# Each weight slab's hi and lo tiles at other places within 256 bytes, low activation parts moved by 64 or 128 bytes

## The chip, the cores and the metric

One NeuronCore of one Trainium2 chip runs the kernel. The metric is device time in microseconds, the median over runs. Engines: PE (TensorE, with PEld for its weight loads), DVE (VectorE), ACT (ScalarE), POOL (GpSimd), SP (SyncE, which issues most DMAs).

## What is computed

One decoder layer for 256 tokens of width 2048, everything in float32:

```
hn = rmsnorm(x)
p  = hn @ w_in + b_in                      # 2048 x 6152
u  = silu(group_norm(causal_dwconv(p[ca] * sigmoid(p[cg]))))
q, k = silu(causal_dwconv(p[q, k])); v, o = p[v], sigmoid(p[o])
hm = group_norm(mlstm(q, k, v, gates)) * o
x  = x + concat(u, hm) @ w_out             # 2048 x 2048
up = rmsnorm(x) @ w_up                     # 2048 x 11264
x  = x + (silu(causal_dwconv(up[gate])) * up[rest]) @ w_down   # 5632 x 2048
out = rmsnorm(x)
```

## The kernel before, in words

Weights stream through SBUF in 400 slabs of 256 rows (two blocks of 128, the index k) by up to 512 columns. SP loads a slab into a tile raw (`load`, L185 on). A float32 slab is then split into two float32r tiles: ACT casts it to hi (L219), and DVE, or POOL for some slabs of the input projection, subtracts to make lo = raw - hi (L224). hi and lo have four buffers each, made in `split_tiles` (L201 on), and are made three slabs ahead of their use. The activations are split in the same way: xp (input projection) and x1p (gate and up) hold high and low parts in one tile, mixh and mixl (output projection) and ah and al (down projection) are two tiles each. A product is then hi x high + hi x low + lo x high, each a float32r matmul with its own weight load on PE.

Which operand streams and which is loaded as weights differs by stage:

- conv gate (slabs 0 to 31) and q and k (56 to 87), `ws_group`, L254: hi or lo is loaded as weights (128 columns), 256 columns of xp stream. 24 matmuls per slab.
- o projection (slabs 32 to 55) and v projection (88 to 103), `xs_group`, L298 to L300: 128 columns of xp are loaded, hi or lo streams, 344 columns for o and 512 for v. 12 matmuls per slab.
- output projection (104 to 135), the same lines: mixh or mixl is loaded, 512 columns of hi or lo stream. 12 per slab.
- gate and up (136 to 311), `wp_group`: hi is loaded and 512 columns of x1p (high and low parts together) stream (L279), then lo is loaded and 256 columns stream (L280). 16 per slab.
- down projection (312 to 399), L298 to L300, and for the last block of columns `down_last` (L850 to L852): ah or al is loaded, 512 columns of hi or lo stream (256 at the very end). 12 per slab.

The order of all instructions is written by hand: a loop over the slabs issues one slab's load, a later slab's split, this slab's matmuls, and the small tasks due at this slab (`after`, `tasks`). The program as built gives each tile a fixed address within a partition. Modulo 256 bytes, all hi and lo tiles start at 160, xp and x1p at 192, mixh, mixl, ah and al at 160. The steps between the column blocks of hi and lo and between the blocks of activations are multiples of 512 bytes, except in the o projection, where the second block of a slab starts 1376 bytes after the first. Parameters come in seven transposed row tiles (`load_rows`, L111 on) with a tag of their own.

Of the kernel before, what the change touches and what calls it, by code (L numbers as in the profile page):

```python
# [9 lines left out]
F32 = mybir.dt.float32  # L10
F32R = mybir.dt.float32r
# [4 lines left out]
P = 128  # L16
# [15 lines left out]
W = 512  # L32

RAW_BUFS = 5
SPLIT_BUFS = 4
AHEAD = 3
SIG = 4
WARM = (6, 5)
BY_K = 3


@with_exitstack
def hybrid_layer_kernel(
# [6 lines left out]
    nc = tc.nc  # L50
    act, dve, pool, pe = nc.scalar, nc.vector, nc.gpsimd, nc.tensor
# [28 lines left out]


    mixh = mid.tile([P, NK, T], F32R, tag="mixh", name="mixh")
    mixl = mid.tile([P, NK, T], F32R, tag="mixl", name="mixl")


# [21 lines left out]
    warm = cst.tile([P, 1], F32, tag="warm", name="warm")  # L107
    act.copy(warm, ones[:, 0:1])

    def load_rows(parts, name):  # L110
        n = sum(p[1] for p in parts)  # L111
        r = mid.tile([P, P], F32, tag="rows", name="rows_" + name, bufs=7)
        o = 0
        for ap, k in parts:
            nc.sync.dma_start(r[o:o + k, :], ap)
            o += k
        return r, n
# [4 lines left out]
    rows = {}  # L122
# [51 lines left out]

    raw_t, hi_t, lo_t = {}, {}, {}
    mid_hook = []

    def load(i):
        if i >= len(slabs):
# [20 lines left out]
    def split_tiles(i):  # L200
        s = slabs[i]  # L201
        n = s["nk"] * s["w"]
        raw = raw_t.pop(i)
        hi = slab.tile([P, 2 * W], F32R, tag="hi", name=f"hi{i}", bufs=SPLIT_BUFS)
        lo = slab.tile([P, 2 * W], F32R, tag="lo", name=f"lo{i}", bufs=SPLIT_BUFS)
        s["eng"] = pool if s["pool"] and i >= 8 and i % 2 else dve
        hi_t[i] = hi[:, :n].rearrange("p (k c) -> p k c", k=s["nk"])
        lo_t[i] = lo[:, :n].rearrange("p (k c) -> p k c", k=s["nk"])
        s["lo"] = 0.0 if s["eng"] is pool else 1.1 * n + 30
        return raw, hi, lo  # L210
# [15 lines left out]
    def w_slab(wap, kt, nk, col, w, fn, on_pool):  # L226
        if col is None:
            src = wap(kt)
        else:
            src = wap[kt * P:(kt + nk) * P, col:col + w].rearrange("(k p) c -> p k c", p=P)  # L230
        slabs.append(dict(src=src, w=w, nk=nk, mm=fn, pool=on_pool))


    def ws_group(wap, col, mov, nk, done, on_pool):
        st = {}

        def mk(kt):
            def fn(hi, lo):
                if kt == 0:
                    st["b"] = [mm_bank("ws0"), mm_bank("ws1")]  # L240
                mh, ml = mov()
                for k in range(2):
                    if mid_hook and mid_hook[0][0] == k:
                        mid_hook.pop(0)[1]()
                    hh, hl, lh = (hi, mh), (hi, ml), (lo, mh)
                    i = cur[0]
                    if i >= NK // 2:
                        steps = [(ct, a) for ct in range(4) for a in (hh, hl, lh)]
                    else:
                        steps = [(ct, a) for a in ((hh, lh, hl) if i + k == 0 else (hh, hl, lh)) for ct in range(4)]  # L250
                    for ct, (w, m) in steps:
                        o = v2(st["b"][ct // 2])[:, ct % 2, :]
                        first = kt + k == 0 and ct % 2 == 0 and w is hi and m is mh
                        pe.matmul(o, w[:, k, ct * P:(ct + 1) * P], m[:, kt + k, :], start=first,  # L254
                                  stop=kt + k == nk - 1 and w is lo, skip_group_check=True)
                if kt + 2 == nk:
                    done(st["b"])
            return fn

        for kt in range(0, nk, 2):  # L260
            w_slab(wap, kt, 2, col, W, mk(kt), on_pool)
# [43 lines left out]
    def xs_group(wap, col, w, stat, nk, done, on_pool):  # L305
        st = {}
        for kt in range(0, nk, 2):
            xs_slab(wap, col, w, stat, kt, kt == 0, kt + 2 == nk, st, done, on_pool)
# [39 lines left out]
    def done_ag(p):  # L348
        def fn(banks):
            sg = []  # L350

            def ev():
                for k in range(2):
                    c = 2 * p + k
                    act.activation(up[c][:, upos:], v2(banks[0])[:, k, :], AF.Identity, bias=bi[:, c:c + 1])
                sg.append(t2k("sg"))
                for k in range(2):
                    c = 2 * p + k
                    act.activation(v2(sg[0])[:, k, :], v2(banks[1])[:, k, :], AF.Sigmoid, bias=bi[:, 8 + c:9 + c])

            def mul():
                for k in range(2):
                    c = 2 * p + k
                    dve.tensor_mul(up[c][:, upos:], up[c][:, upos:], v2(sg[0])[:, k, :])
                conv_pair(p)
            d0 = 5 if p == 0 else 1
            after(d0, lambda: scale_banks(banks), 1300)
            after(d0 + 1, ev)
            after(d0 + 2, mul, 700)
        return fn  # L370
# [312 lines left out]
    def open_ffn():  # L683
        if "ah" in ffn:
            return
        inner.close()
        fp = ctx.enter_context(tc.tile_pool(name="ffn", bufs=1))
        ffn["pool"] = fp
        ffn["ah"] = fp.tile([P, NF, T], F32R, tag="ah", name="ah")
        ffn["al"] = fp.tile([P, NF, T], F32R, tag="al", name="al")  # L690
        ffn["gp"] = [fp.tile([P, 2, FK - 1 + T], F32, tag=f"gp{i}", name=f"gp{i}") for i in range(2)]
        for g in ffn["gp"]:
            pool.memset(g[:, :, 0:FK - 1], 0.0)
# [194 lines left out]


    ag = w_in[:, 0:2 * DC].rearrange("(k p) (s c) -> p k s c", p=P, s=2)  # L890
    for j in range(4):
        ws_group(lambda kt, j=j: ag[:, kt:kt + 2, :, T * j:T * (j + 1)], None, get_xT, NK, done_ag(j), True)
    for b in range(3):
        xs_group(w_in, OFF_O + OW * b, OW, get_xT, NK, done_o(b), True)
    for half in range(2):
        ws_group(w_in, OFF_Q + 512 * half, get_xT, NK, done_qk(0, half), True)
        ws_group(w_in, OFF_K + 512 * half, get_xT, NK, done_qk(1, half), True)

    at = defaultdict(list)
    v_start = len(slabs)  # L900
    for hp in range(2):
        xs_group(w_in, OFF_V + 512 * hp, W, get_xT, NK, done_v(hp), True)
    at[v_start - 2] += [(0, 0), (1, 1)]
# [3 lines left out]
        return mixh, mixl  # L907

    p3_start = len(slabs)
    sts = [{}, {}, {}, {"cv": True}]  # L910
    for n0 in (0, 2):
        for half in range(2):
            for n in (n0, n0 + 1):
                for kt in range(8 * half, 8 * half + 8, 2):
                    xs_slab(w_out, 512 * n, W, get_mix, kt, kt == 0, kt == 14, sts[n], done_out(n), False)

    for j in range(NF // 4):
        wp_group(w_up, 512 * j, done_gate(j), gate_banks)
        wp_group(w_up, DFF + 512 * j, done_up(j), up_banks)
    for n in range(3):  # L920
        xs_group(w_down, 512 * n, W, lambda: (ffn["ah"], ffn["al"]), NF, done_down(n, 512 * n, W), False)
    down_last(3, 1536, W, SPLIT_BUFS)
# [189 lines left out]
```

## Time and profile before

| | us |
|---|---|
| median of 2 runs | 1130.84 (1130.81 to 1130.87) |
| the profiled execution | 1131.08 |
| its span, first to last instruction | 1129.3 |
| PE busy, mean granted clock | 1118.7, 0.998 |
| DVE, ACT, POOL busy | 746.0, 578.9, 131.6 |

The profile is of one execution. Busy time on PE is no measure of its rate, since matmuls are pipelined; the distance between the starts of matmuls is.

### The profile page before, as it was taken

Reading aid. Unit: us, or ns where it says so; the run is one execution under the profiler, and the core shown is the slowest. Engines: PE = TensorE matmul, PEld = TensorE weight load, DVE = VectorE, ACT = ScalarE, POOL = GpSimd, SP = SyncE. Lnnn points to the kernel's source line nnn. Section 1 sums busy time; section 2 is a strip of 40 time slices with the busy share of each in tenths; the row PEclk is TensorE's granted clock in tenths of the full one; section 3 lists DMA queues with packets and bytes.
Section 4 is the critical chain, followed back from the end, with each engine's and each line's share of the span. In section 5 each row is a group of like instructions: output and inputs, shape, how many; then the busy total and the mean of one; then the engine's idle time right before and its main releaser. Section 6 shows DMA issues by size and latency. Waiting matters only on the chain.

```text
span 1129.3 us, 16955 instructions
## 1 busy us (share of the span) xinstructions
PE 1118.7 (99%) x6506; PEld 994.4 (88%) x6506; DVE 746.0 (66%) x1139; ACT 578.9 (51%) x823; POOL 131.6 (12%) x100
## 2 busy tenths in 40 slices
PE   9999999999999999999999999999999999999997
PEld 9999999998888888888888888888888888888886
DVE  5498999986765557657666666676576645454543
ACT  5745476754545455555545555455555444343433
POOL 0443554534200000000000000000000000000000
PEclk9999999999999999999999999999999999999999
DMA  8864665565655666666666666666666666666662
GB/s 262 272 190 125 193 205 186 175 183 166 218 192 184 173 195 190 192 188 185 188 199 191 184 191 189 194 188 192 188 186 188 197 193 230 197 188 196 191 195 89
DMA packets 122681, 215.40 MB, mean 191 GB/s; under 512 B 7440, under 2 KB 33256, under 8 KB 122088
## 3 DMA queue, kind: packets, MB, share of 16 engines
q1 hardware_dynamic: 121048, 209.92, 61.8%
q10 hardware_dynamic: 1552, 4.39, 1.0%
q8 instruction: 51, 0.84, 0.3%
q14 instruction: 30, 0.25, 0.1%
HBM read 212.19 MB, written 2.10 MB: 190 GB/s over the span
## 4 chain that ended last, share of the span: by engine, by line
PE 95%; DVE 3%; ACT 1%; issue 1%; DMA 0%; ACTq 0%; POOLq 0%; POOL 0%
PE ws L254 16%; PE gate L279 14%; PE up L279 14%; PE xs L298 9%; PE xs L299 9%; PE xs L300 9%; PE up L280 8%; PE gate L280 8%; PE xs L852 2%; PE xs L850 2%; PE xs L851 2%; DVE conv L386 2%; DVE lo L224 1%; DMA xs<-in_x_dram 0%; PE xT L940 0%
## 5 line engine op out<-in xcount | busy, mean ns | idle before, releaser
L224 DVE TENSOR_TENSOR lo<-raw,hi 128x1024 fp32r<-128x1024 f32 (+2 forms) x355 | 434.6, 1225 | 326.6 <-ACT hi L219 325.5
L219 ACT CAST hi<-raw 128x1024 fp32r<-128x1024 f32 (+2 forms) x401 | 411.5, 1030 | 452.4 <-PE xs L300 152.5
L279 PE MATMUL gate<-x1p,hi 128*128 128x512 f32 x704 | 245.0, 390 | 0.0
L279 PE MATMUL up<-x1p,hi 128*128 128x512 f32 x704 | 244.5, 390 | 0.0
L280 PE MATMUL up<-x1p,lo 128*128 128x256 f32 x704 | 198.5, 282 | 0.0
L280 PE MATMUL gate<-x1p,lo 128*128 128x256 f32 x704 | 198.5, 282 | 0.0
L254 PE MATMUL ws<-xp,hi 128*128 128x256 f32 x1024 | 178.5, 282 | 0.0
L279 PEld LDWEIGHTS up<-x1p,hi 128*128 128x128 f32 x704 | 132.2, 188 | 27.7
L279 PEld LDWEIGHTS gate<-x1p,hi 128*128 128x128 f32 x704 | 132.2, 188 | 27.6
L254 PEld LDWEIGHTS ws<-xp,hi 128*128 128x128 f32 x1024 | 153.4, 189 | 0.8 <-issue 0.3
L254 PE MATMUL ws<-xp,lo 128*128 128x256 f32 x512 | 135.5, 280 | 0.5 <-DVE lo L224 0.5
L280 PEld LDWEIGHTS gate<-x1p,lo 128*128 128x128 f32 x704 | 133.1, 189 | 0.0
L280 PEld LDWEIGHTS up<-x1p,lo 128*128 128x128 f32 x704 | 133.1, 189 | 0.0
L224 POOL TENSOR_TENSOR lo<-raw,hi 128x1024 fp32r<-128x1024 f32 (+1 forms) x48 | 111.1, 2317 | 148.2 <-ACT hi L219 142.2
L299 PE MATMUL xs<-lo,ah 128*128 128x512 f32 x264 | 102.7, 389 | 0.0
L300 PE MATMUL xs<-hi,al 128*128 128x512 f32 x264 | 102.7, 389 | 0.0
L298 PE MATMUL xs<-hi,ah 128*128 128x512 f32 x264 | 102.7, 389 | 0.0
L386 DVE SCALAR_TENSOR_TENSOR conv<-up,cB,conv 128x256 f32<-128x256 f32 x240 | 97.6, 478 | 0.0
L254 PEld LDWEIGHTS ws<-xp,lo 128*128 128x128 f32 x512 | 93.2, 189 | 0.9 <-DVE lo L224 0.7
L827 POOL TENSOR_TENSOR rf<-ms,halves 128x1 f32<-128x1 f32 x2 | 1.1, 550 | 711.7 <-DVE ms L821 711.7
L300 PEld LDWEIGHTS xs<-hi,al 128*128 128x128 f32 x264 | 49.6, 188 | 10.4
L298 PEld LDWEIGHTS xs<-hi,ah 128*128 128x128 f32 x264 | 49.6, 188 | 10.4
(186 smaller groups left out, 1204.5 us busy)
## 6 DMA issues: line engine op xcount, KB each, us to landing
raw<-in_w_up_dram SPq DMA_DIRECT2D x176, 512.0 KB, 3.9
raw<-in_w_down_dram SPq DMA_DIRECT2D x88, 512.0 KB, 4.7
raw<-in_w_in_dram SPq DMA_DIRECT2D x48, 512.0 KB, 4.4
raw<-in_w_in_dram SPq DMA_DIRECT2D x64, 256.0 KB, 4.6
raw<-in_w_out_dram SPq DMA_DIRECT2D x32, 512.0 KB, 4.6
raw<-in_w_in_dram SPq DMA_DIRECT2D x24, 344.0 KB, 3.4
x<-in_x_dram ACTq DMA_DIRECT2D x2, 1024.0 KB, 7.7
xs<-in_x_dram SPq DMA_DIRECT2D x7, 256.0 KB, 5.6
```

Of the source, the lines that this page charges most:

```text
L219: copy(hi[:, c], raw[:, c])
L224: slabs[i]["eng"].tensor_sub(lo[:, c], raw[:, c], hi[:, c].bitcast(F32))
L254: pe.matmul(o, w[:, k, ct * P:(ct + 1) * P], m[:, kt + k, :], start=first, stop=kt + k == nk - 1 and w is lo, skip_group_check=True)
L279: pe.matmul(o, hi[:, k, cs], m2, start=first, stop=last, skip_group_check=True)
L280: pe.matmul(o[:, 0:T], lo[:, k, cs], mp[:, kt + k, 0, :], start=False, stop=last, skip_group_check=True)
L298: pe.matmul(o, sh[:, kt + k, ts_], hi[:, k, :w], start=first and k == 0, stop=False)
L299: pe.matmul(o, sh[:, kt + k, ts_], lo[:, k, :w], start=False, stop=False)
L300: pe.matmul(o, sl[:, kt + k, ts_], hi[:, k, :w], start=False, stop=last and k == 1)
L386: dve.scalar_tensor_tensor(a, up[c][:, t:t + T], cB[:, 8 * t + c:8 * t + c + 1], a, op0=ALU.mult, op1=ALU.add)
L850: pe.matmul(o, sh[:, kt, ts_], hi[:, k, c:c + cw], start=kt == first, stop=False, skip_group_check=True)
L851: pe.matmul(o, sh[:, kt, ts_], lo[:, k, c:c + cw], start=False, stop=False, skip_group_check=True)
L852: pe.matmul(o, sl[:, kt, ts_], hi[:, k, c:c + cw], start=False, stop=kt == NF - 1, skip_group_check=True)
```

## The change

The tiles hi and lo get 64 spare elements (256 bytes), and each slab uses its hi and lo from an offset of its own within them. `place(base, *pairs)` sets for the slabs that follow a list of pairs (bytes for hi, bytes for lo) through which they go in turn; the base is 32 where the partner is xp or x1p and 0 where it is mixh or ah, so that a pair tells how many bytes, modulo 256, hi and lo lie behind that partner. Before, the pair is (224, 224) for stages with xp or x1p, and (0, 0) for the two others.

- conv gate, q and k: (192, 64) in every slab; o projection: (64, 64); v projection: (0, 0)
- output projection: the 32 pairs of MID, one per slab
- gate and up: the last 176 of the 192 pairs of ALL, one per slab: all multiples of 16 of which at least one is no multiple of 32
- down projection: the 88 pairs of MORE, one per slab

A tile gap of 16 elements stands between mixh and mixl, and one of 32 between ah and al, each with a memset on POOL: mixl now starts at 224 and al at 32, modulo 256. To make room, the row tiles of the parameters take thirds of the tiles pw, which the mLSTM scores use later.

```
     mixh = mid.tile([P, NK, T], F32R, tag="mixh", name="mixh")
+    gap = mid.tile([P, 16], F32, tag="gap", name="gap")
+    nc.gpsimd.memset(gap, 0.0)
     mixl = mid.tile([P, NK, T], F32R, tag="mixl", name="mixl")

+    row_tiles = []
     def load_rows(parts, name):
-        r = mid.tile([P, P], F32, tag="rows", name="rows_" + name, bufs=7)
+        if not row_tiles:
+            t = mid.tile([P, 384], F32, tag="pw", name="rows_" + name, bufs=4)
+            row_tiles.extend(t[:, c * P:(c + 1) * P] for c in (2, 1, 0))
+        r = row_tiles.pop()

+    def place(base, *pairs):
+        stage["base"], stage["from"], stage["pairs"] = base, len(slabs), pairs
+
+    def places():
+        h, l = stage["pairs"][(len(slabs) - stage["from"]) % len(stage["pairs"])]
+        return (stage["base"] + h) % 256 // 4, (stage["base"] + l) % 256 // 4
+
+    G16 = [16 * a for a in range(16)]
+    ALL = [(h, l) for h in G16 for l in G16 if h % 32 or l % 32]
+    MID = [(h, l) for h in (0, 64, 128, 192) for l in (0, 32, 64, 96, 128, 160, 192, 224)]
+    MORE = [(h, l) for h in (0, 16, 32, 64, 128, 144, 160, 192) for l in (0, 16, 32, 64, 80, 128, 144, 160, 192, 208, 240)]

-        hi = slab.tile([P, 2 * W], F32R, tag="hi", name=f"hi{i}", bufs=SPLIT_BUFS)
-        lo = slab.tile([P, 2 * W], F32R, tag="lo", name=f"lo{i}", bufs=SPLIT_BUFS)
+        hi = slab.tile([P, 2 * W + ROOM], F32R, tag="hi", name=f"hi{i}", bufs=SPLIT_BUFS)
+        lo = slab.tile([P, 2 * W + ROOM], F32R, tag="lo", name=f"lo{i}", bufs=SPLIT_BUFS)
+        hi, lo = (t[:, o:o + 2 * W] for t, o in zip((hi, lo), s["at"]))

-        slabs.append(dict(src=src, w=w, nk=nk, mm=fn, pool=on_pool))
+        slabs.append(dict(src=src, w=w, nk=nk, mm=fn, pool=on_pool, at=places()))

         ffn["ah"] = fp.tile([P, NF, T], F32R, tag="ah", name="ah")
+        gap = fp.tile([P, 32], F32, tag="gap", name="gap")
+        pool.memset(gap, 0.0)
         ffn["al"] = fp.tile([P, NF, T], F32R, tag="al", name="al")

+    place(FROM_X, (192, 64))        # conv gate
+    place(FROM_X, (64, 64))         # o
+    place(FROM_X, (192, 64))        # q, k
+    place(FROM_X, (0, 0))           # v
+    place(FROM_MIX, *MID)           # output
+    place(FROM_X, *ALL[16:])        # gate, up
+    place(FROM_MIX, *MORE)          # down
```

No instruction of PE, ACT, DVE or SP is added or moved; two of the four writes of pw on DVE now also name a DMA queue among their waits. On POOL the two memsets are added. The program before, POOL's first instructions of the kernel proper (ident is the identity for PE's transposes):

```order
L1107 UNCONDITIONAL_BRANCH
masks.py:197 MEMSET ident 128x128
masks.py:199 ISA
masks.py:199 AFFINE_SELECT ident<-ident 128x128
L322 MEMSET up_98 128x30
```

And the changed program at the same place:

```order
L1141 UNCONDITIONAL_BRANCH
L86 MEMSET gap 128x16
masks.py:197 MEMSET ident 128x128
masks.py:199 ISA
masks.py:199 AFFINE_SELECT ident<-ident 128x128
L347 MEMSET up_100 128x30
```

The memset of gap stands ahead of ident; the rest follows as before.

## Rows read from the trace of the kernel before

**Rows 1.** The page: span, busy time, granted clock in 40 slices (9: 90% or more).

```profile
span 1129.3 us, 16955 instructions
...
PE 1118.7 (99%) x6506; PEld 994.4 (88%) x6506; DVE 746.0 (66%) x1139; ACT 578.9 (51%) x823; POOL 131.6 (12%) x100
...
PEclk9999999999999999999999999999999999999999
```


**Rows 2.** Waits of PE: us in total, times, longest; first and last of four.

```profile
PE warm L968 <- POOL ident masks.py:199: 1.4, 1, 1.4
...
PE xs L299 <- DVE lo L224: 0.4, 1, 0.4
```


**Rows 3.** Stretches: us, busy (instructions) by engine, granted clock, DMA share, GB/s.

```profile
98.00:150.00 52.00, 51.09 (x339) 50.58 (x338) 46.80 (x109) 28.96 (x43) 24.32 (x16) 1.00 0.61 180
150.00:245.60 95.60, 95.60 (x801) 94.00 (x802) 89.92 (x185) 63.95 (x90) 47.80 (x28) 1.00 0.61 188
...
391.00:883.00 492.00, 492.00 (x2841) 436.11 (x2840) 329.44 (x444) 261.11 (x385) 1.93 (x4) 1.00 0.65 190
```


**Rows 4.** Timeline of PE, down projection: start, us, engine, line; 12 steps apart.

```profile
1081.68 0.39 PE L850 MATMUL xs<-hi,ah 128*128 128x512 f32 x1
...
1084.40 0.39 PE L850 MATMUL xs<-hi,ah 128*128 128x512 f32 x1
```


**Rows 5.** Timeline of PE, end of the down projection; 24 steps apart.

```profile
1115.68 0.28 PE L850 MATMUL xs<-hi,ah 128*128 128x256 f32 x1
...
1118.56 0.28 PE L850 MATMUL xs<-hi,ah 128*128 128x256 f32 x1
```


**Rows 6.** Timeline of PE, up projection; 16 steps apart.

```profile
469.91 0.39 PE L279 MATMUL up<-x1p,hi 128*128 128x512 f32 x1
...
472.68 0.39 PE L279 MATMUL up<-x1p,hi 128*128 128x512 f32 x1
```


**Rows 7.** Timeline of PE, q and k; 24 steps apart.

```profile
231.90 0.39 PE L254 MATMUL ws<-xp,hi 128*128 128x256 f32 x2
...
234.70 0.39 PE L254 MATMUL ws<-xp,hi 128*128 128x256 f32 x2
```


**Rows 8.** Timeline of PE, o projection; 24 steps apart.

```profile
120.87 0.32 PE L298 MATMUL xs<-hi,xp 128*128 128x344 f32 x1
...
124.62 0.32 PE L298 MATMUL xs<-hi,xp 128*128 128x344 f32 x1
```


**Rows 9.** Timeline of PE, v projection; 12 steps apart.

```profile
251.30 0.40 PE L298 MATMUL xs<-hi,xp 128*128 128x512 f32 x1
...
254.10 0.40 PE L298 MATMUL xs<-hi,xp 128*128 128x512 f32 x1
```


**Rows 10.** Timeline of PE, the scores, in plain float32.

```profile
241.69 1.02 PE L570 MATMUL S<-qkt 128*128 128x256 f32 x4
```


**Rows 11.** Groups by shape: line, tiles, count | busy us, mean ns | idle before.

```profile
L279 PE MATMUL gate<-x1p,hi 128*128 128x512 f32 x704 | 245.0, 390 | 0.0
...
L280 PE MATMUL gate<-x1p,lo 128*128 128x256 f32 x704 | 198.5, 282 | 0.0
L254 PE MATMUL ws<-xp,hi 128*128 128x256 f32 x1024 | 178.5, 282 | 0.0
...
L254 PE MATMUL ws<-xp,lo 128*128 128x256 f32 x512 | 135.5, 280 | 0.5 <-DVE lo L224 0.5
...
L570 PE MATMUL S<-qkt 128*128 128x256 f32 x16 | 4.1, 378 | 0.0
```


**Rows 12.** Groups from 391 to 883 us: the casts and the subtractions.

```profile
L224 DVE TENSOR_TENSOR lo<-raw,hi 128x1024 fp32r<-128x1024 f32 x178 | 217.6, 1223 | 159.6 <-ACT hi L219 159.5
...
L219 ACT CAST hi<-raw 128x1024 fp32r<-128x1024 f32 x178 | 186.8, 1051 | 214.6 <-PE gate L279 114.9 <-PE up L279 91.2 <-ACT s L741 6.9
```


**Rows 13.** Timeline of the start: POOL's memsets and the second transposes of x.

```profile
1.32 0.53 POOL L322 MEMSET up<- 128x30 f32 x8
...
5.46 0.66 PE L940 MATMUL xT<-ident,xs 128*128 128x128 f32 x2 [0.54 <-DMA xs<-in_x_dram]
```

More of the change, by code (lines that the diff above doesn't have):

```diff
@@ L39 @@
 BY_K = 3
+ROOM = 64
+FROM_X, FROM_MIX = 32, 0
 @with_exitstack
@@ L176, in hybrid_layer_kernel @@
     mid_hook = []
+    stage = {}
+    def place(base, *pairs):
[7 more added lines that the diff above has]
+    MORE = [(h, l) for h in (0, 16, 32, 64, 128, 144, 160, 192) for l in (0, 16, 32, 64, 80, 128, 144, 160, 192, 208, 240)]
     def load(i):
```

## The prediction

> **What bounds the kernel now.** I read the page first. TensorE (PE) is busy 99% of a span of 1129.3 us, its granted clock is full in all 40 slices, and no other engine passes 66% [rows 1]. The waits of PE come next: four rows, from 1.4 us at the start down to 0.4 us [rows 2]. Then the stretches [rows 3]: PE is busy nearly all of the time in each (51.09 of 52.00, 95.60 of 95.60, 492.00 of 492.00 us) at a granted clock of 1.00, the 2.4 GHz level; VectorE (DVE) is near full from 98 to 150 us (46.80 of 52.00) and from 150 to 245.6 us (89.92 of 95.60), and two thirds busy in gate and up. So the time is the sum of the matmuls' steps, and the question is how long a step is. A matmul's own duration (390 ns) says nothing, since matmuls are pipelined; the step from one start to the next does, so the timelines of PE are read last, first and last row of a run with the count between.
>
> Every float32r matmul loads new weights, so a step is the streamed columns plus something for that load. In the down projection twelve steps of 512 columns take 1084.40 - 1081.68 = 2.72 us, 226.7 ns each [rows 4]; at its end 24 steps of 256 columns take 2.88 us, 120.0 ns each [rows 5]. The difference, 106.7 ns for 256 columns, is one column per cycle at 2.4 GHz, and the remainder is 13.3 ns in both: I call it the gap. The gap by stage:
> - gate and up: 16 matmuls (eight of 512, eight of 256 columns) in 472.68 - 469.91 = 2.77 us, 173.3 ns each against 160.0 of columns: 13.3 ns [rows 6]
> - conv gate, q and k (L254): 24 of 256 columns in 234.70 - 231.90 = 2.80 us, 116.7 ns: 10.0 ns [rows 7]
> - o projection: 24 of 344 columns in 3.75 us, 156.2 ns against 143.3: 12.9 ns [rows 8]
> - v projection: 12 of 512 columns in 2.80 us, 233.3 ns: 20.0 ns [rows 9]
> - scores, in plain float32: four of 256 columns, start of the first to end of the last 1.02 us, one lasting 0.38: three steps in 0.64 us, some 214 ns; if two cycles go to a column (213.3 ns) the gap is some 1 ns [rows 10, 11].
>
> So the gap isn't one constant. The kernel as built puts hi and lo at byte 160 of 256, xp and x1p at 192, mixh, mixl, ah and al at 160. Projection v streams hi and lo past weights 32 bytes further on; the down projection does the same at distance 0 with the same shapes, and its gap is 6.7 ns smaller. This pair of rows is the one sign in the trace that places matter; that v runs beside the mLSTM is the other explanation. Gate (distance 224, gap 13.3) and L254 (distance 224, gap 10.0) show that the distance alone does not settle it.
>
> **The change part by part.** No instruction of PE, ACT or SP is added, removed or moved; only addresses are new. The steps that it touches: gate and up 4 x 704 = 2816 (L279 and L280, each for gate and for up; two of the four rows in [rows 11]), output 32 slabs x 12 = 384, down 1080 (three column blocks of 22 slabs x 12, the last block 288 with its halves), v 16 x 12 = 192, o 24 x 12 = 288, L254 1024 + 512 = 1536 [rows 11].
>
> 1. Gate and up. Each of the 176 slabs gets another pair out of (16, 128) to (240, 240), relative to x1p, at least one of the two off the multiples of 32. No row shows such a place. Bounds from the nearest rows: the gap of the scores, 1 ns, gives 2816 x -12.3 = -34.6 us; that of v, 20 ns, gives 2816 x 6.7 = +18.9 us. A mean over 176 pairs that run through the 256 bytes should lie where most rows lie, 10 to 13.3 ns; I take 13.3, the row of this very stage: 0.
> 2. Output and down. hi in four (output) or eight (down) places, lo in eight or eleven, and the low part of the activations 64 (mixl) or 128 (al) bytes behind. 1464 steps, now at 13.3 ns. Bounds as above: 1464 x -12.3 = -18.0 us and 1464 x 6.7 = +9.8 us. I take 13.3, since 36 of 88 pairs in down and all 32 in output stay on multiples of 32: 0.
> 3. Projection v. hi and lo go to the place of xp, distance 0, as in the down projection [rows 4]. 192 x (13.3 - 20.0) = -1.3 us. If the mLSTM beside it makes the gap, 0; if it falls to 1 ns, -3.6 us.
> 4. L254 (conv gate, q, k): hi 192 and lo 64 bytes behind xp in place of 224 both. No row shows these distances. Bounds: 1536 x -9 = -13.8 us and 1536 x 10 = +15.4 us. I take no change, 0. For q and k half of a gain would be lost: DVE is idle only 95.60 - 89.92 = 5.7 us there [rows 3] and makes most of the lo tiles.
> 5. o projection: hi and lo 64 bytes behind xp, 288 x (1 - 12.9) = -3.4 us to 288 x 7.1 = +2.0 us; DVE is idle 5.2 us of the 52.0 there [rows 3], and PE already waits for its lo once [rows 2], so a small gain can show as that wait. I take 0.
> 6. ACT and DVE write hi and lo at other places. In gate and up the cast takes 1051 ns and the subtraction 1223 ns per slab of 2.77 us [rows 12], off the path. The cover goes when DVE, busy 329.44 of 492.00 us [rows 3], gets 162.6 us more work over 178 slabs, 0.91 us each, so the subtraction would have to slow from 1.22 to 2.1 us. Cost 0.
> 7. Two memsets on POOL. The first stands ahead of ident, for which PE's warm-up waits; the eight memsets of 128x30 take 0.53 us, so one of 128x16 some 0.06 us. The first transposes go on to wait for x by DMA, 0.54 us at 5.46 us [rows 13], which hides it. The second, before gp's memsets in the first gate group, has no reader, and nothing stands behind it on POOL but gp's two and the last two rf. Cost 0.
> 8. The rows of parameters share the pw tiles; two of the scores' four writes also wait for a DMA of rows, which landed some 200 us before. Cost 0.
>
> Sum: -1.3 us on the profiled 1131.08 us (span 1129.3 and 1.8 around it) is 1129.8 us; against the median, 1130.84, it is 1129.5 us. That is the forecast: no change that counts. A measurement of this kernel can tell about 2%, 22.6 us, from no change; in gaps, 4280 steps of gate, up, output and down by 5.3 ns.
>
> [...]
>
> [...]
>
> **The rivals.**
> - A, slower: the places off the multiples of 32 meet the other stream more often. All gate and up steps and the 52 of 88 down slabs with such a place go to v's 20 ns: 2816 x 6.7 + 1080 x 52/88 x 6.7 = 18.9 + 4.3 = +23.2 us, 1154 us. It becomes slower by over 2% where these stages' mean gap passes 18.6 ns. For it: v's row shows that 20 ns occurs at a distance of only 32 [rows 9]. Against: in v every step has that one distance, and here each slab has another.
> - B, faster: the gap is a collision of weight load and stream which most places avoid, as the scores' 1 ns suggests [rows 10]. If half of the pairs avoid it: half of (34.6 + 18.0) = -26.3 us, with v's -1.3 us 1103 us. Against: the scores stream at half the rate, and no float32r row is under 10 ns.
> - C, the change does nothing: the gap is a fixed price of a float32r weight load, and v's is the mLSTM's doing. 1130.8 us. Against: the same shapes give 20.0 and 13.3 at a steady step in both.
>
> **How the numbers follow.** Forecast, places matter but average out: 0.58. C: 0.17. A: 0.12. B: 0.13. Forecast and C lie within 2%, 0.75; B is the chance of faster by over 2%, A of slower. Inside the forecast the mean gaps may lie 4 ns to either side: 4280 x 4 = 17 us, with L254's 5 us of gain or loss about 20 us. So the range is 1108 to 1150 us; it leaves out the far parts of A and B, some 0.18.
>
> **What would show it.** Right: gate slabs whose 16 steps differ from slab to slab, around 2.77 us in the mean; v at 2.72 us per slab; PE 99% busy and the four waits as before. Wrong: all gate slabs at 2.77 us still (C), a mean under 2.69 us (B) or over 2.86 us (A); or new waits of PE for lo, which would mean that ACT or DVE became slow at the new places. The prediction fails if the time is off by more than 20 us, or if v stays at 2.80 us, since then its one term that rests on a row is wrong.

## The result, and the profile after

The changed kernel takes 1139.45 us (two runs, 1138.45 to 1140.45) against 1130.84 before: 1.0079 times as long, 95% interval 1.0058 to 1.0099. That is 8.6 us more: less than the 2% that count as a change, but well outside the scatter. The forecast of "no change" missed a small, real loss.

The page of the changed kernel: span, busy time, granted clock in 40 slices.

```profile
span 1138.7 us, 16959 instructions
...
PE 1127.8 (99%) x6506; PEld 991.4 (87%) x6506; DVE 741.8 (65%) x1139; ACT 578.4 (51%) x823; POOL 133.4 (12%) x102
...
PEclk9999999999999999999999999999999999999999
```

Against [rows 1] the span is 9.4 us longer and PE busy 9.1 us longer, with the same 6506 matmuls and the granted clock full in every slice. So the time went into PE's steps. The waits of PE (us in total, times, longest; all but the second and third row) and the stretches (us; busy time and instructions of PE, PEld, DVE, ACT, POOL; granted clock, DMA share, GB/s) show that PE does not wait for the other engines:

```profile
PE warm L1002 <- POOL ident masks.py:199: 1.5, 1, 1.5
...
PE ws L279 <- POOL lo L249: 0.5, 1, 0.5
PE xs L324 <- DVE lo L249: 0.3, 1, 0.3
```

```profile
98.00:150.00 52.00, 51.73 (x344) 51.41 (x344) 46.80 (x117) 28.33 (x43) 27.24 (x17) 1.00 0.60 181
150.00:246.00 96.00, 96.00 (x806) 94.58 (x806) 86.92 (x179) 65.01 (x91) 47.31 (x27) 1.00 0.60 187
392.70:886.10 493.40, 493.40 (x2829) 431.66 (x2828) 328.94 (x441) 258.53 (x379) 1.99 (x5) 1.00 0.65 188
```

The longest wait is 1.5 us, 1.4 in [rows 2], and there are five rows in place of four. Gate and up (the last stretch) fill PE without a break at a clock of 1.00, as in [rows 3]. The casts and subtractions there last what they did in [rows 12]:

```profile
L249 DVE TENSOR_TENSOR lo<-raw,hi 128x1024 fp32r<-128x1024 f32 x177 | 216.5, 1224 | 162.0 <-ACT hi L244 161.9
L244 ACT CAST hi<-raw 128x1024 fp32r<-128x1024 f32 x177 | 185.5, 1049 | 217.2 <-PE gate L304 117.2 <-PE up L304 91.2 <-ACT s L768 7.1
```

1224 and 1049 ns, against 1223 and 1051. What is left is the gap. The timeline of PE in the changed kernel, first row of a slab and first row of the next (start, us, engine, line); the lines L279, L304 and L323 were L254, L279 and L298:

```profile
166.62 0.39 PE L279 MATMUL ws<-xp,hi 128*128 128x256 f32 x2
...
169.34 0.28 PE L279 MATMUL ws<-xp,hi 128*128 128x256 f32 x1
...
206.88 0.40 PE L279 MATMUL ws<-xp,hi 128*128 128x256 f32 x2
...
209.73 0.28 PE L279 MATMUL ws<-xp,hi 128*128 128x256 f32 x1
...
252.40 0.39 PE L323 MATMUL xs<-hi,xp 128*128 128x512 f32 x1
...
255.12 0.39 PE L323 MATMUL xs<-hi,xp 128*128 128x512 f32 x1
...
494.64 0.39 PE L304 MATMUL gate<-x1p,hi 128*128 128x512 f32 x1
...
497.36 0.39 PE L304 MATMUL gate<-x1p,hi 128*128 128x512 f32 x1
...
584.18 0.40 PE L304 MATMUL gate<-x1p,hi 128*128 128x512 f32 x1
...
587.00 0.40 PE L304 MATMUL gate<-x1p,hi 128*128 128x512 f32 x1
...
936.09 0.39 PE L323 MATMUL xs<-hi,ah 128*128 128x512 f32 x1
...
938.86 0.39 PE L323 MATMUL xs<-hi,ah 128*128 128x512 f32 x1
```

Read them as the prediction does, steps minus 0.417 ns a column: 256 columns more take 106.7 ns from [rows 5] to [rows 4], 2.4 columns a ns, at a granted clock of 1.00. All gaps are worked out with this estimate. The two slabs of q and k have the same pair, (192, 64), and yet take 2.72 and 2.85 us: 6.7 and 12.1 ns against 10.0 in [rows 7]. The v slab takes 2.72 us, 13.3 ns against 20.0 in [rows 9]. The two gate slabs, pairs (64, 144) and (112, 64), take 2.72 and 2.82 us: 10.0 and 16.3 ns, on either side of the 13.3 of [rows 6]. The down slab, pair (16, 160), takes 2.77 us for its twelve steps, 17.5 ns against 13.3 in [rows 4].

The same reading over every float32r step (starts of all matmuls; steps with a gap over 40 ns are left out) gives the mean gap by stage, in ns, for both kernels and for eight of the twelve that the experiments add; the other four hold several places in a stage and are read slab by slab. The time of e8 and of e12 is that of one run.

| | L254 | o | v | output | gate, up | down | us |
|---|---|---|---|---|---|---|---|
| steps | 1536 | 288 | 192 | 384 | 2816 | 1080 | |
| before | 10.4 | 13.0 | 19.7 | 14.0 | 13.35 | 13.3 | 1130.84 |
| after | 10.3 | 14.0 | 14.7 | 18.2 | 14.75 | 17.9 | 1139.45 |
| e1_low_parts_back | 9.3 | 14.0 | 14.6 | 18.1 | 14.75 | 17.8 | 1139.61 |
| e2_low_parts_only | 10.1 | 12.9 | 19.8 | 17.6 | 13.3 | 17.6 | 1137.00 |
| e3_input_places_only | 9.3 | 14.0 | 14.6 | 14.1 | 13.35 | 13.3 | 1129.11 |
| e4_one_pair_in_gate | 10.3 | 13.1 | 14.7 | 14.0 | 10.0 | 13.4 | 1120.58 |
| e6_l254_at_64_64 | 7.6 | 13.0 | 14.7 | 14.1 | 10.0 | 13.4 | 1117.77 |
| e8_all_64_further | 10.4 | 12.9 | 14.7 | 14.2 | 15.0 | 13.4 | 1134.76 |
| e11_one_pattern | 8.2 | 13.0 | 14.4 | 14.0 | 10.05 | 13.4 | 1118.69 |
| e12_one_pattern_moved | 9.2 | 12.9 | 14.7 | 14.2 | 10.0 | 13.4 | 1120.26 |

After minus before, steps times gap: gate and up 2816 x 1.4 = +3.9 us, down 1080 x 4.6 = +5.0, output 384 x 4.1 = +1.6, o +0.3, v 192 x -5.0 = -1.0, L254 about 0. The sum, +9.8 us, is the span's +9.4. So the question for the experiments: does a pair of places fix the gap of its own steps, or does it cost to go from one pair to another at every slab, and which of the edits did it?

### The profile page after: what moved, and what is told of

It reads as the page before. It is cut to its first block, busy times and chain, and to the rows that moved or that the text cites. A ratio compares the mean times of both kernels' runs of the same rounds, so it can differ in the third digit from the quotient of the medians.

```text
span 1138.7 us, 16959 instructions
## 1 busy us (share of the span) xinstructions
PE 1127.8 (99%) x6506; PEld 991.4 (87%) x6506; DVE 741.8 (65%) x1139; ACT 578.4 (51%) x823; POOL 133.4 (12%) x102
## 4 chain that ended last, share of the span: by engine, by line
PE 93%; DMA 3%; DVE 1%; ACT 1%; issue 1%; SPq 1%; POOL 0%; ACTq 0%; POOLq 0%; DVEq 0%
PE up L304 14%; PE gate L304 14%; PE ws L279 12%; PE xs L324 10%; PE xs L325 10%; PE xs L323 10%; PE up L305 7%; PE gate L305 7%; PE xs L877 2%; PE xs L879 2%; PE xs L878 2%; DMA raw<-in_w_in_dram 2%; DMA bb<-in_b_in_dram 1%; DVE conv L411 1%; SPq L214 0%
## 5 line engine op out<-in xcount | busy, mean ns | idle before, releaser
L304 PE MATMUL gate<-x1p,hi 128*128 128x512 f32 x704 | 246.8, 394 | 0.0
L304 PE MATMUL up<-x1p,hi 128*128 128x512 f32 x704 | 246.7, 394 | 0.0
L279 PE MATMUL ws<-xp,hi 128*128 128x256 f32 x1024 | 178.0, 282 | 0.0
L304 PEld LDWEIGHTS up<-x1p,hi 128*128 128x128 f32 x704 | 132.1, 188 | 31.0
L304 PEld LDWEIGHTS gate<-x1p,hi 128*128 128x128 f32 x704 | 132.2, 188 | 30.6
L279 PEld LDWEIGHTS ws<-xp,hi 128*128 128x128 f32 x1024 | 152.4, 188 | 0.8 <-issue 0.3
L279 PE MATMUL ws<-xp,lo 128*128 128x256 f32 x512 | 135.0, 279 | 0.5 <-POOL lo L249 0.5
L323 PE MATMUL xs<-hi,ah 128*128 128x512 f32 x264 | 103.9, 394 | 0.0
L279 PEld LDWEIGHTS ws<-xp,lo 128*128 128x128 f32 x512 | 93.0, 189 | 0.7 <-POOL lo L249 0.7
L323 PEld LDWEIGHTS xs<-hi,ah 128*128 128x128 f32 x264 | 49.6, 188 | 11.5
```

The lines of the kernel that those rows point to most:

```text
L304: pe.matmul(o, hi[:, k, cs], m2, start=first, stop=last, skip_group_check=True)
L323: pe.matmul(o, sh[:, kt + k, ts_], hi[:, k, :w], start=first and k == 0, stop=False)
```

## The experiments

The study ran twelve kernels. Ratios are to runs of the kernel before on the same chip. Edits are cut to the lines that matter; every gap tile has its memset, which is left out. "Held" means that a pair stays for several slabs, "single" that it has one slab. Down's gaps are those of its 512-column steps, unless 256 columns are named.

**1. The low parts back where they were.** The change without its two gap tiles.

```
-    gap = mid.tile([P, 16], F32, tag="gap", name="gap")
-        gap = fp.tile([P, 32], F32, tag="gap", name="gap")
```

> The changed kernel without the two gap tiles: mixl and al start at 160 again, as mixh and ah do; all pairs of places stay. Theory S (the shifted low parts cost what the output and down projections lost: a mean gap of 18.15 ns and 17.94 ns in the changed kernel against 14.0 and 13.3 before): their gaps return to about 14 and 13.5 ns, 374 + 1077 steps by some 4.5 ns, 6.6 us less than the changed kernel's 1139.45, so about 1133 us. Theory P (the places of the slabs, or their change from slab to slab, cost it): both gaps stay near 18 ns and the time near 1139.5 us.

1139.61 us, ratio 1.0072 (1.0056 to 1.0088). Down's slab (16, 160) again, timeline of PE, 12 steps:

```profile
935.76 0.40 PE L321 MATMUL xs<-hi,ah 128*128 128x512 f32 x1
...
938.57 0.39 PE L321 MATMUL xs<-hi,ah 128*128 128x512 f32 x1
```

2.81 us, 20.8 ns, where the low parts 128 bytes off gave 17.5: single slabs move up and down, the mean doesn't (17.8 and 17.9). The places of hi and lo alone cost the whole loss.

**2. The low parts moved, nothing else.** The kernel before with the two gap tiles.

```
+    gap = mid.tile([P, 16], F32, tag="gap", name="gap")
+        gap = fp.tile([P, 32], F32, tag="gap", name="gap")
```

> The kernel before with the two gap tiles alone: mixl 64 and al 128 bytes behind, every slab's hi and lo at 160 as before. Theory S: gaps of about 18 ns in the output and down projections, some 6.6 us more than before, about 1137.5 us. Theory P: gaps of 14.0 and 13.3 ns as before, 1130.8 us. In both, gate and up stay at 13.3 ns and v at 20.0 ns.

1137.0 us, ratio 1.0051 (1.0033 to 1.0069). Timeline of PE, a down slab; nearly all slabs of the first three column blocks read alike:

```profile
933.28 0.39 PE L300 MATMUL xs<-hi,ah 128*128 128x512 f32 x1
...
936.05 0.39 PE L300 MATMUL xs<-hi,ah 128*128 128x512 f32 x1
```

2.77 us, 17.5 ns: steady, with no change of place between slabs. So this edit alone, too, costs nearly the whole loss in output and down, and the two don't add up. What both leave is the condition of before.

Nor does the loss come from other engines that read and write SBUF at the same time. Near the end of down no other engine runs for 2.8 us and no DMA moves data, in the kernel before (first row) as in this one (second row; columns as above):

```profile
1112.80:1115.60 2.80, 2.80 (x14) 2.33 (x13) 0.00 (x0) 0.00 (x0) 0.00 (x0) 1.00 0.00 0
...
1119.20:1122.00 2.80, 2.80 (x15) 2.30 (x14) 0.00 (x0) 0.00 (x0) 0.00 (x0) 1.00 0.00 0
```

The steps there keep their gaps, 13.3 ns before and 17.7 ns here, so neither value needs another engine's traffic.

**3. Places of the input projection only.** Gate and up, output and down as before.

```
-    place(FROM_MIX, *MID)
+    place(FROM_MIX, (0, 0))
-    place(FROM_X, *ALL[16:])
+    place(FROM_X, (224, 224))
-    place(FROM_MIX, *MORE)
+    place(FROM_MIX, (0, 0))
```

(and no gap tiles.)

> The changed places in the input projection alone (conv gate, o, q, k, v); gate and up at (224, 224), output and down at (0, 0), no gap tiles, so that these have their places of before. If place alone makes v's gap: 13.3 ns per undisturbed step in v, 20.0 before, about -1.1 us. If the conv gate, q and k steps fall into one of two repeating patterns (the changed kernel showed 6.7 and 12.2 ns with the same places), each of their 64 slabs shows either 2.72 or 2.85 us, and the time lies between 1130.8 - 1.1 - 8 = 1122 us and 1132 us, depending on how many slabs are in each; gate, up, output and down as before at 13.3 to 14 ns. If instead the patterns were an effect of the later stages' places, all of them would be at 10.0 ns, as before.

1129.11 us, ratio 0.9982 (0.9973 to 0.9992): v's gain is real and the loss is gone. Of the time saved, v's gap gives 1.0 us; some 1.7 us come from L254, which had 9.3 ns in the mean in this run. v's undisturbed slabs read 13.3 ns beside the same mLSTM, so that was not v's cause. L254 shows its two gaps, 6.7 and 12.2 ns, at one pair.

**4. One pair in gate and up.** The third kernel with the cheapest pair of the changed kernel's sweep held in all 176 slabs, and o back at (224, 224).

```
-    place(FROM_X, (64, 64))
+    place(FROM_X, (224, 224))
-    place(FROM_X, (224, 224))
+    place(FROM_X, (64, 144))
```

> As the one with the input places only, but gate and up hold the pair (64, 144) in all 176 slabs, the pair whose slab had the smallest gap in the changed kernel (10.0 ns), and the o projection is back at (224, 224). Theory H (the gap belongs to the pair, and holding it keeps the pattern): gate and up at about 10.0 ns, 2.72 us per slab, 2816 steps by 3.3 ns, 9.4 us less than with the input places only. Theory T (one slab's gap is a passing state after the neighbour's places): gate and up settle at 13 ns or more, no gain.

1120.58 us, ratio 0.9905 (0.9889 to 0.992). Timeline of PE, 16 steps of gate:

```profile
567.20 0.39 PE L302 MATMUL gate<-x1p,hi 128*128 128x512 f32 x1
...
569.92 0.39 PE L302 MATMUL gate<-x1p,hi 128*128 128x512 f32 x1
```

2.72 us, 10.0 ns, the value that the pair had in its one slab. 2816 x 3.3 = 9.3 us less in gate and up, of which L254's patterns take back some 1.5 us (10.3 ns for 9.3). The kernel beats both.

**5. Pairs held for eight slabs.** Whether the pair or the change of pair costs.

```
-    place(FROM_MIX, (0, 0))
+    place(FROM_MIX, *[p for p in ((160, 160), (32, 160), (16, 80), (192, 192), (192, 208), (192, 240),
+          (64, 64), (128, 64), (0, 0), (192, 16), (192, 192)) for _ in range(8)])
```

(down; alike in the other stages.)

> This kernel keeps the activations where they were before (no gap tiles) and holds each pair for eight slabs in every stage, so that one slab in eight has a change ahead of it. In gate and up six pairs are held (mean gap in the changed kernel, one slab each: (112,128) 17.1, (96,16) 16.4, (16,208) 17.0, (80,144) 17.0, (208,80) 12.6, (176,0) 12.9 ns), then 128 further pairs stand one slab each. In down the pairs held are (160,160), (32,160), (16,80), (192,192), (192,208), (192,240), (64,64), (128,64), (0,0), (192,16), (192,192); one slab each in the kernel with only the low parts moved back they had 20.8, 19.8, 18.9, 12.4, 13.9, 13.0, 15.5, 15.5, 13.3 (held), 15.6. Theory H (the pair itself sets the gap of every step): all eight slabs of a held group show the value that the pair had alone, within 0.5 ns, so gate's six groups read 17.1, 16.4, 17.0, 17.0, 12.6, 12.9, and down's from 12.4 to 20.8. Theory T (going from one place to another costs, and a held pair settles at some 13.3 ns whichever it is): the first slab of each group is dear, the seven behind it lie at 13 to 13.5, and the single pairs lie at 14 to 17. For L254 (eight groups of eight) H says each group has one gap between 6.7 and 12.2 ns; if that stage has two patterns for any pair, groups jump between the two at interruptions as with (192,64). For o and v: (0,0) 13.3 in v, another value for (192,192) in its second half under H. Time: not the point; some 1130 to 1140 us under either.

1142.43 us, one run. Gate's six pairs read 16.3, 17.3, 16.6, 16.7, 12.3 and 13.3 ns over their eight slabs, against 17.1, 16.4, 16.5, 17.0, 12.6 and 12.9 alone. Down's read 20.9, 20.0, 18.9, 20.0, 19.2, 18.9, 15.6, 15.6, 13.3, 13.3 and, for (192, 192) again, 20.0. Timeline of PE, third slab of (32, 160) and third of (192, 16):

```profile
916.73 0.39 PE L321 MATMUL xs<-hi,ah 128*128 128x512 f32 x1
...
919.53 0.39 PE L321 MATMUL xs<-hi,ah 128*128 128x512 f32 x1
...
1094.04 0.39 PE L873 MATMUL xs<-hi,ah 128*128 128x512 f32 x1
...
1096.76 0.39 PE L873 MATMUL xs<-hi,ah 128*128 128x512 f32 x1
```

2.80 and 2.72 us: 20.0 and 13.3. Theory T falls: a dear pair stays dear. H's 0.5 ns was too narrow (gate's groups lie up to 0.9 ns off).

The last four slabs, all at (192, 192), show one thing more: the first six steps of each have 512 columns and read 20.0 ns, and the twelve that are left for the end have 256. Timeline of PE, 24 steps apart:

```profile
1127.50 0.28 PE L873 MATMUL xs<-hi,ah 128*128 128x256 f32 x1
...
1130.22 0.28 PE L873 MATMUL xs<-hi,ah 128*128 128x256 f32 x1
```

2.72 us, 113.3 ns a step: 6.7 ns at the same pair. So the gap depends on the columns that stream, too: 256 columns more take 120.0 ns here, and 106.7 at (0, 0) [rows 4, 5], the pair from which the 0.417 ns a column is estimated. (192, 192), (192, 208) and (192, 240) were expected to be cheap because their single slabs are among the last four, where both kinds of steps were averaged. The first slab of down's first ten groups lies 0.6 ns above the later ones in the mean (from 1.6 below to 3.3 above), a small part of the 4.6. In v, (192, 192) reads 20.0 where (0, 0) reads 13.3. In L254, (64, 64) reads 6.7 to 7.1 in all eight slabs.

**6. L254 at (64, 64).** The fourth kernel with that pair in conv gate, q and k.

```
-    place(FROM_X, (192, 64))
+    place(FROM_X, (64, 64))
```

> The kernel with gate and up held at (64,144) (1120.58 us), with one difference: conv gate, q and k (L254) hold (64,64) in place of (192,64). Theory H (a pair has its own gap in each stage): L254 takes 6.7 ns in all 64 slabs, as it did in the eight slabs that held (64,64), against a mean of 10.3 before; 1536 x 3.6 = 5.5 us less on PE. In q and k half of that is lost to waits for lo, since DVE is near full there, and the first slabs wait for DMA, so 2.5 to 5 us less: 1115.5 to 1118 us. Rival (that stage has two patterns whichever pair it holds, and the eight slabs were luck): slabs at 6.7 and at 12.2 mixed, some 10 ns in the mean, 1120 to 1121 us.

1117.77 us, ratio 0.9886 (0.987 to 0.9903), the fastest kernel. Most slabs read 6.7 ns, but seven of q and k's first eight don't. Timeline of PE, a slab of conv gate and one of q and k:

```profile
66.65 0.39 PE L277 MATMUL ws<-xp,hi 128*128 128x256 f32 x2
...
69.37 0.28 PE L277 MATMUL ws<-xp,hi 128*128 128x256 f32 x1
...
159.63 0.40 PE L277 MATMUL ws<-xp,hi 128*128 128x256 f32 x2
...
162.46 0.28 PE L277 MATMUL ws<-xp,hi 128*128 128x256 f32 x1
```

2.72 and 2.83 us, 6.7 and 11.3 ns, with one pair. Neither theory had it whole: the mean (7.6) is near H's, and the two gaps are the rival's.

**7. Pairs held with the low parts 128 bytes off.** Gap tiles of 32 elements in both stages.

```
+    gap = mid.tile([P, 32], F32, tag="gap", name="gap")
+        gap = fp.tile([P, 32], F32, tag="gap", name="gap")
-    place(FROM_MIX, (0, 0))
+    place(FROM_MIX, *[p for p in ((64, 128), (0, 240), (192, 16), (144, 16), (64, 144), (160, 208),
+          (0, 160), (128, 0), (144, 144), (16, 240), (0, 0)) for _ in range(8)])
```

(down; the pairs of the other stages are left out.)

> Gap tiles of 32 elements stand between mixh and mixl and between ah and al, so the low parts lie 128 bytes off in both stages; pairs are held for eight slabs in output and down. In down: (64,128), (0,240), (192,16), (144,16), (64,144), (160,208), (0,160), (128,0), (144,144), (16,240), (0,0); in the changed kernel, one slab each, these had 14.6, 14.4, 14.3, 15.2, 15.5, 15.5, 15.4, 15.5, 15.5, 15.9, 18.5. H: each group has one gap in its slabs two to eight, at most 1 to 2 ns under the value of its single slab, (0,0) at 17.6 as in the run with only the low parts moved; output's (64,0), (128,128), (128,64), (0,128) read as the same pairs in down would. If a pair with the low parts apart goes under 13.3 ns there is something to gain in 1464 steps. The rival, that 13.3 is the least these shapes allow, says none does. Gate and up go through 176 pairs in steps of four bytes around (64,144): H says between 10 and 21 ns, and some others at 10.0 or under.

1139.85 us, one run. Down reads 14.4, 22.2, 13.3, 17.7, 17.7, 15.5, 13.3, 15.5, 15.6, 18.3 and, for (0, 0), 17.7. The dearest, (0, 240), timeline of PE:

```profile
914.70 0.40 PE L323 MATMUL xs<-hi,ah 128*128 128x512 f32 x1
...
917.53 0.40 PE L323 MATMUL xs<-hi,ah 128*128 128x512 f32 x1
```

2.83 us, 22.5 ns, where its single slab in the changed kernel had 14.4. That is a miss of the expectation: in down a single slab can lie up to 8 ns off its pair's steady value. None goes under 13.3. In gate and up the 176 pairs around (64, 144) lie between 10.0 and 19.7 ns, none under 10.0. Output's pair (0, 128), where lo lies as far behind mixl as it did before, reads 17.7: putting that one distance back isn't enough.

**8. All 64 bytes further.** The fourth kernel with both operands of output and down moved together.

```
-FROM_X, FROM_MIX = 32, 0
+FROM_X, FROM_MIX = 32, 64
+    gap = mid.tile([P, 16], F32, tag="gap", name="gap")
     mixh = mid.tile([P, NK, T], F32R, tag="mixh", name="mixh")
+        gap = fp.tile([P, 16], F32, tag="gap", name="gap")
         ffn["ah"] = fp.tile([P, NF, T], F32R, tag="ah", name="ah")
```

> The kernel with gate and up held at (64,144), with mixh, mixl, ah, al, hi and lo all 64 bytes further on in output and down: the distances between the two operands are those of before, the places modulo 256 are others. If the distances alone decide, output and down stay at 14.0 and 13.3 ns and the time at 1120 to 1121.5 us. If the place of each in itself decides (a place modulo 256 that is good or bad for loading weights or for streaming), the two stages go to another value, as likely 15 to 20 ns as not: up to 1464 x 6.7 = 9.8 us more. v, o and L254 are as in that kernel.

1134.76 us, one run, and neither answer as expected. Timeline of PE, a gate slab and a down slab:

```profile
571.85 0.40 PE L304 MATMUL gate<-x1p,hi 128*128 128x512 f32 x1
...
574.65 0.40 PE L304 MATMUL gate<-x1p,hi 128*128 128x512 f32 x1
...
934.44 0.39 PE L323 MATMUL xs<-hi,ah 128*128 128x512 f32 x1
...
937.16 0.39 PE L323 MATMUL xs<-hi,ah 128*128 128x512 f32 x1
```

Down stays at 2.72 us, 13.3 ns: there the distances decide, not the place of each by itself (shown for one shift). The 14 us come from gate and up, 2.80 us or 15.0 ns in nearly every slab, although no address there differs from the fourth kernel's.

**9. The same places entered anew.** Each held place is entered many times out of one slab at another place.

```
-    place(FROM_X, (64, 144))
+    place(FROM_X, *[e for x in [(0, 0), (208, 80), (176, 0), (224, 224), (112, 128), (16, 208), (80, 144),
+          (96, 16), (32, 32), (128, 128), (64, 160), (160, 96), (192, 48), (240, 240)] for e in [x] + [(64, 144)] * 7],
+          *[e for x in [(0, 0), (208, 80), (64, 144), (112, 128), (16, 208), (96, 16), (128, 128), (192, 48)]
+          for e in [x] + [(224, 224)] * 7])
```

(gate and up; alike in the other stages.)

> In the run with everything in output and down 64 bytes further on, gate and up went to 15.0 ns in all slabs although their own addresses were those of the run that showed 10.0. This kernel enters the same place many times, each time out of one slab at another place: in gate and up 14 times seven slabs at (64,144), then eight times seven at (224,224), the place of before; in down eleven times, in output four times and in v twice seven slabs at (0,0); in L254 eight times seven at (64,64); in o three times seven at (224,224). Theory H2 (some places have two repeating patterns, and what stood ahead of the first steps chooses): the 14 groups at (64,144) read 10.0 or 15.0, each of them throughout its seven slabs; L254's groups read 6.7 or 11.1; those at (224,224) in gate and (0,0) in down read one value, 13.3, whatever they were entered from. Theory H (one gap for each place, and something else differed in that run): all 14 at 10.0, all of L254's at 6.7. A third way (another condition of the chip in that execution): 15.0 in all 14 or drifting within a group. Time: not the point, some 1120 to 1135 us.

1130.26 us, one run. Of the 14 groups at (64, 144), five settle at 10.0 ns and nine at 15.0, and each stays there to its end. Timeline of PE, a slab of each kind, and one of (224, 224):

```profile
446.63 0.39 PE L302 MATMUL gate<-x1p,hi 128*128 128x512 f32 x1
...
449.43 0.39 PE L302 MATMUL gate<-x1p,hi 128*128 128x512 f32 x1
...
535.53 0.39 PE L302 MATMUL gate<-x1p,hi 128*128 128x512 f32 x1
...
538.25 0.39 PE L302 MATMUL gate<-x1p,hi 128*128 128x512 f32 x1
...
713.35 0.39 PE L302 MATMUL gate<-x1p,hi 128*128 128x512 f32 x1
...
716.12 0.39 PE L302 MATMUL gate<-x1p,hi 128*128 128x512 f32 x1
```

2.80, 2.72 and 2.77 us. All eight groups at (224, 224) settle at 13.3, and all eleven of down at (0, 0). L254 at (64, 64) settles near 6.7 in seven groups of eight and at 11.1 in one. H2's first half holds: some places have two repeating patterns. That the steps ahead choose between them is not shown, since no entry was repeated with the same slab ahead.

**10. Other places.** Five further pairs in gate and up, each entered eight times, and 22 pairs held in down.

```
-    place(FROM_X, (64, 144))
+    place(FROM_X, *[e for p in [(64, 0), (64, 132), (64, 156), (52, 144), (208, 80)]
+          for x in [(0, 0), (208, 48), (112, 128), (16, 208), (96, 16), (128, 128), (192, 48), (240, 240)]
+          for e in [x, p, p, p]], *[e for x in [(0, 0), (112, 128)] for e in [x] + [(176, 0)] * 7])
```

(gate and up; the pairs of the other stages are left out.)

> (64,144) in gate and up has two patterns (10.0 and 15.0 ns, five and nine of 14 groups). This kernel looks for a place with one pattern below 13.3: in gate and up it enters each of (64,0), (64,132), (64,156), (52,144) and (208,80) eight times out of one slab at eight other places and holds it three slabs, then (176,0) twice for seven. Theory H2 with the four near ones as neighbours of one pattern: they too split into 10.0 and 15.0 or thereabouts; (208,80) reads 12.3 in all eight, the value that it had when held. If one of the four reads 10.0 in all eight groups, it is the better choice. In down 22 further pairs are held four slabs each, with the low parts where they were before, eight in output, L254 16, o six, v four: if any of down's 22 lies under 13.3 there is a gain of up to 1464 x 6.6 = 9.7 us left there; the theory that 13.3 is the least for these shapes (eighteen pairs held so far, at either distance of the low parts, none below) says none does. Time: not the point, some 1130 to 1140 us.

1138.05 us, one run. (64, 132), (64, 156) and (52, 144) settle at 10.0 in all eight entries (10.0 to 10.3 in the third held slab); (208, 80) at 12.1 in seven and 16.6 in one; (64, 0) at 10.0 in one and near 15 in most. (176, 0) reads 15.9 in one entry and 16.7 in the other, where the fifth kernel had held it at 13.3: a value that has stood for eight slabs is no proof that a place has only that one. Timeline of PE, a slab of (64, 132):

```profile
493.12 0.39 PE L302 MATMUL gate<-x1p,hi 128*128 128x512 f32 x1
...
495.84 0.39 PE L302 MATMUL gate<-x1p,hi 128*128 128x512 f32 x1
```

In down the 22 pairs lie at 15.5 to 21.1 ns (with 256 columns (64, 128), the last, has 11.2). With the ten of the fifth kernel that makes 32 pairs held at the old distance of the low parts: mean 18.4, two at 13.3, (0, 0) and (192, 16), none under it. For 23 of these pairs the first kernel has a single slab as well: their mean is 18.3 held and 18.2 single, so going to another pair at every slab costs nothing in the mean. The changed kernel, with its low parts apart, has 18.2 in the mean over the 88 pairs.

**11 and 12. A place with one pattern.** The sixth and the eighth kernel with gate and up at (64, 132).

```
-    place(FROM_X, (64, 144))
+    place(FROM_X, (64, 132))
```

> The kernel with L254 at (64,64), with gate and up held at (64,132) in place of (64,144). Both give 10.0 ns once the pattern of 10.0 is there, so H2 expects the same time, 1117 to 1119 us, and 10.0 ns in the slabs from the sixth on. If eight entries of three slabs were too few to show a second pattern of (64,132), it could settle at 15 ns, some 14 us more, 1132 us.

> The run with everything in output and down 64 bytes further on, in which gate and up at (64,144) fell into 15.0 ns and the time was 1134.76 us; here gate and up hold (64,132), nothing else differs. If (64,132) has one pattern, gate and up read 10.0 ns and the time falls by 2816 x 5 = 14 us to some 1120.7 us. If what stands ahead of gate and up there makes any place dear, they stay near 15.0 ns and 1134 us.

1118.69 us, ratio 0.9888 (0.987 to 0.9906), not to be told from the sixth kernel; and 1120.26 us (one run) where (64, 144) had 1134.76. The sixth and the eleventh kernel are the same program up to gate and up, and yet q and k's slabs 23 to 31 read 6.7 ns in the sixth and 11.1 in the eleventh: which pattern L254 fell into differed between these two executions. A gate slab of the twelfth, timeline of PE:

```profile
566.29 0.39 PE L304 MATMUL gate<-x1p,hi 128*128 128x512 f32 x1
...
569.01 0.39 PE L304 MATMUL gate<-x1p,hi 128*128 128x512 f32 x1
```

2.72 us in place of 2.80.

## Why the prediction was wrong

The time lies 10 us above the forecast, inside its range, but it went the other way: 8.6 us more where 1.3 less was forecast. The signs that the prediction named came true (gate slabs from 2.72 to 2.83 us, v at 2.72, PE 99% busy), so "places matter but average out" holds in its first half. The second half, what the average is, failed.

- **The failed step is term 2**, output and down at 0, "I take 13.3, since 36 of 88 pairs in down and all 32 in output stay on multiples of 32". Measured: +6.6 us. Two things were wrong in it. Multiples of 32 are no safe class: in the changed kernel down's 512-column steps have 18.6 ns at the 36 pairs with both offsets on multiples of 32 and 18.0 at the other 52. And the value of before was taken for a typical one. It was the lowest that down's 512-column steps show in any run here: of 32 pairs held, two reach 13.3 and the mean is 18.4. Leaving it could only lose, and a mean over pairs is what the changed kernel got. The low parts moved by themselves lose as much (17.6), and the two edits together lose no more than one.
- **Term 1**, gate and up at 0, was mis-sized by +1.4 ns in 2816 steps, +3.9 us. Here "a mean over 176 pairs that run through the 256 bytes should lie where most rows lie, 10 to 13.3 ns" failed by a little: the pairs have 14.75, from 10.0 to 17, and before's 13.35 was below the middle, not the floor.
- **Term 3**, v: -1.3 forecast, -1.0 measured. The one term that rested on two rows of the same shapes was right, its cause too: its undisturbed slabs have exactly 13.3, the mean is 14.7 because slabs just behind the mLSTM's small matmuls have 14 to 18.
- **Term 4**, L254: 0 forecast, about 0 measured, by luck: the stage is at 6.7 or at 12.2 ns by turns, and the mean happens to be before's (the first and the third kernel, with the same places in L254, have 9.3). The prediction's 10.0 was read in q and k alone; in the kernel before, 18 of conv gate's 32 slabs have 11.1.
- **Terms 5 to 8**: o lost 0.3 us (14.0 for 13.0); casts, subtractions, memsets and rows cost nothing that can be seen, as said (in gate and up 1049 and 1224 ns against 1051 and 1223; PE's longest wait 1.5 us against 1.4).
- **The rivals.** C falls: the gap follows the places. With the same instructions and shapes the gap of down's held pairs went from 13.3 to 22.2 ns, so it is no fixed price of a float32r weight load, and v's fell from 19.7 to 14.7 ns beside the same mLSTM. A had the sign and a part of the size, but its class of dear places does not show: in down the 52 pairs off the multiples of 32 have 18.0 ns, the 36 on them 18.6. B was right that some pairs have less of the gap (10.0 ns at (64, 144) in gate and up, 6.7 at (64, 64) in L254), though no pair goes under 10.0 in gate and up or under 13.3 in down's 512-column steps, and a kernel that runs through all pairs gets the mean, not the best. That a collision of weight load and stream makes the gap was its author's guess; no run shows what does.

In short: that places matter was right; the averaging was wrong by 4 to 5 ns in output (14.0 to 18.2) and down (13.3 to 17.9), where before has the lowest mean in the table.

## What to carry to other kernels

Where PE's steps are back to back and each loads new weights, measure the gap of each stage; if it differs between like shapes, sweep the distance of the two operands in one kernel (here over 256 bytes; no run tried another span), hold each pair for several slabs, and then hold the best in all of them: here the eleventh kernel gains 12.3 us (1.1%). Don't average over what a search could choose, and before leaving a value ask where it stands among its alternatives. Test a good place by entering it out of several others, since here gate and up at (64, 144), which has two patterns, took 14 us more after an edit of other stages (1134.76 us against 1120.58, one run).

## What was not expected of the hardware

- The gap of a steady float32r step takes values that recur: 6.7, 10.0, 11.1, 12.2, 13.3, 15.0, 15.5, 16.7, 17.7, 18.9, 20.0 ns. Four or eight bytes further a slab can read another: (64, 132) has 10.0 in all its eight entries, while (64, 136) and (64, 140) had 15.8 and 13.4 in a slab of their own. At (64, 144) the value is the mean of a pattern that repeats: the steps of gate and up have 14 and 6 ns by turns in the fourth kernel (10.0), and 21, 10, 18, 11 in the eighth (15.0).
- At the same addresses the gap can settle at one of two values: (64, 144) at 10.0 or 15.0, L254 at (64, 64) at 6.7 or 11.1, at (192, 64) at 6.7 or 12.2, at (224, 224) at 10.0 or 11.1. It keeps the value, in gate and up over 170 slabs. L254 in the changed kernel kept 12.2 over 430 steps in a row (48.7 to 99.7 us), and went from 6.7 (up to 183.2 us) to 12.2 (from 184.1) where small matmuls stood between. What chooses is open. In L254 it is not the program alone (6.7 and 11.1 ns in slabs 23 to 31 of q and k in the sixth and the eleventh kernel, the same program up to there). In gate and up the four runs of the fourth kernel lie within 2 us of each other and so do those of the sixth, so (64, 144), where 15.0 takes 14 us more, stayed at 10.0 in all eight of them; the eighth kernel, at 15.0, had one run.
- What makes a pair cheap is open, and it depends on the columns: (192, 192) in down has 20.0 ns with 512 and 6.7 with 256. In down the distances decide and not each place by itself (13.3 and 13.4 ns in the mean before and after both moved by 64 bytes, eighth kernel, one shift), but not one distance alone: with hi at 0 from the high part and lo at 0 from the low part, output settles at 13.3 where the two parts are at one place (before) and at 17.7 where they lie 128 bytes apart (seventh kernel).
